# First modulation stream in tiles of 1024 columns, first softmax's factor applied to the output by ScalarE

## The chip, the core and the metric

The kernel runs on one core of a Trainium2 chip. The core has TensorE (PE in the profile), VectorE (DVE), ScalarE (ACT), GpSimd (POOL), SyncE (SP, which here only issues transfers) and 16 DMA engines that bring data from the device's memory. The engines run their own instruction streams, each in its own fixed order, and wait for one another by semaphores. Matmuls are full fp32 in value but are done as three products of rounded halves, so the three matmul lines 188, 189 and 190 always come together.

The metric is the device time of one execution in microseconds. Lower is better.

## What is computed

A trunk of two layers on 512 tokens of width 2048. The first has differential attention with eight heads, the second forgetting attention with sixteen. Each layer takes three modulation vectors of 2048 (shift, scale, gate) from a conditioning vector; the shared keys and values take two more. Cut to what the change touches:

```
c_act = silu(c)                                   # 2048
mod = c_act @ w_mod[l] + b_mod[l]                 # 3 x 2048: shift, scale, gate
mod = c_act @ w_mod_kv + b_mod_kv                 # 2 x 2048: shift, scale of the shared k, v

p = softmax(sc)                                   # per head two softmaxes, (query, key)
a = p[:, :, 0] - lam * p[:, :, 1]
o = a @ v                                         # 256 wide
o = rms_norm(o, subln_g) * (1.0 - lam_init)
o = o * silu(g)
```

## The kernel before, in words

**Projections.** The input of a layer stands transposed in 16 pairs of tiles (`hh`, `hl`: high and low half, 128 features by 512 tokens). A weight of 2048 by 512 columns is a job of eight sub-steps. For each sub-step SP loads 256 rows (`wst`), ACT rounds them to the high half (`whi`, line 108) and DVE subtracts to get the low half (`wlo`, line 109). `group` (line 318) then runs, for each sub-step, four bursts of six matmuls, one burst per accumulator bank: 32 bursts per group. With the last sub-step each bank is emptied by `evac`, right after its last burst. There are four accumulator banks, and the next group uses the same four in the same order.

**Order of the groups in the first layer.** A start phase, then `kk` and head 2's q/k group `qk[2]`, head 2's v/gate group `vg[2]`, and for heads 3 to 7 each a q/k group and a v/gate group (lines 908 to 949), then the output projection (line 1083). In time: `qk[2]` begins at 222 us, `vg[2]` ends at 329, head 4's v/gate group ends at 524, head 5's at 622, head 6's at 720, head 7's at 817. The attention of head h - 1 runs beside the groups of head h as a list of pieces; `tick` (line 302) takes one piece after each burst. `drain` takes what is left of them at once, before the first bank of a group is emptied.

**Emptying a v/gate bank** (`evac_vg`, line 716): ACT rounds v to `vh`, DVE makes `vl`, ACT takes a tanh (`th`), DVE makes `sg` (line 728). `sg` is the last reader of the bank.

**Attention of a head** (`attention_a`, line 731). `score` makes the scores of 128 queries for one of the two softmaxes, DVE adds the bias and takes the row's bound, ACT the exponent and the row sum (`e`, line 758, `rsum`). When both are there, DVE takes the reciprocals of the two sums, multiplies the second by `neglam`, multiplies the first `e` by its factor (line 765) and adds the second times its own (line 766). `e` is then transposed, either by PE (heads 0, 1 and 7) or by DVE and two trips through memory (`turn_small`, `send`, `take`). `values` multiplies by v into the bank `o`; for every two blocks of queries `norm` (line 827) copies `o` to `og`, takes the sum of squares, the reciprocal root on DVE (three rounds of tiny instructions) and scales by it and `sg` (line 839). `store` transposes `og` on PE (line 853).

**The modulation stream** (`mod_stream`, line 387) makes vectors in the background of the groups. It is a generator; `tick` takes `bg` steps of it after a burst. Here it makes four vectors, the gate of layer 0, shift and scale of the shared k and v, and the shift of layer 1, each 16 row tiles by four segments of 512 columns. One load (`ms`, line 400) brings 256 rows of a segment, two row tiles; there are two buffers, and a load is issued just ahead of the sums of the tile before it. Each step is one sum on DVE: `macc` = weights x activation (line 422 for the first row tile) or `macc` += (line 424). The sums of a stream are kept in program order. When a segment is whole, `mod_rows` (line 442) reduces over the 128 partitions: a transpose in blocks of 32 (`mturn`, line 452) and a reduction (`mred`, line 453), at step 1 of the next segment; after the fourth segment comes a matmul with ones (line 462), an add of the bias and a store, at step 5.

Steps per group before: in `qk[2]` every third burst (10 of 32), in `vg[2]` every second (16), in the q/k groups of heads 3 to 7 two of three (21), in their v/gate groups three of four (24), in the first part of the output projection one after each burst. What is left then is done at once in `open_n`.

The same generator is used a second time in layer 1 (line 1193), with segments of 512 columns.

**Order.** The kernel is written in program order, and a planner sets at build time the order in which each engine gets its instructions; it may put an instruction ahead of earlier ones that it holds to be not ready. On the chip each engine's order is then fixed.

Of the kernel before, what the change touches and what calls it, by code (L numbers as in the profile page):

```python
# [16 lines left out]
P = 128  # L17
# [107 lines left out]
def tile_yoco(  # L125
# [261 lines left out]
    def mod_stream(segs, new_stage, new_acc, nk, deep=0, new_deep=None):  # L387

        todo = [(i, r) for i in range(len(segs)) for r in range(KT // nk)]
        loaded = {}
        summed = []

        def load(k):
            i, r = todo[k]
            src, col, _ = segs[i]
            t = new_deep() if k < deep else new_stage()
            rows = src[nk * r * P : nk * (r + 1) * P, col : col + 512]
            nc.sync.dma_start(t, rows.rearrange("(k p) n -> p k n", p=P) if nk > 1 else rows)  # L400
            loaded[k] = t

        def load_upto(k):
            n = len(loads)
            while n < len(todo) and n <= (k + 7 if n < deep else k + 2 // nk):
                load(n)
                loads.append(n)
                n += 1

        loads = []  # L410
        load_upto(-1)
        for k, (i, r) in enumerate(todo):
            load_upto(k)
            if r == 0:
                acc = new_acc()
            t = loaded.pop(k)
            for kk in range(nk):
                kt = nk * r + kk
                w = t[:, kk, :] if nk > 1 else t

                if kt == 0:
                    ins = V.tensor_scalar(acc, w, cact[:, 0:1], None, op0=ALU.mult)
                else:
                    ins = V.scalar_tensor_tensor(acc, w, cact[:, kt : kt + 1], acc, op0=ALU.mult, op1=ALU.add)  # L424
                tc.keep_in_program_order(ins)
                if kt == KT - 1:
                    summed.append(segs[i][2](acc))
                if kt in (1, 5) and summed:
                    if next(summed[0], None) is None:
                        summed.pop()  # L430
                yield
        for _ in summed[0]:
            yield
# [8 lines left out]
    def mod_rows(pool, fours, dst, bias, one):  # L442
# [5 lines left out]
        def steps(n, acc):  # L448
            if n == 0:
                red.append(pool.tile([P, 64], F32, name="mred", tag="mred", bufs=2))  # L450
            t = pool.tile([P, 512], F32, name="mturn", tag="mturn", bufs=1)
            V.transpose(t, acc)
            V.tensor_reduce(
                red[0][:, 16 * n : 16 * n + 16], t.rearrange("p (j q) -> p j q", q=32), axis=mybir.AxisListType.X, op=ALU.add
            )
            if n == 3:
                row = pool.tile([64, 32], F32, name="mrow", tag="mrow", bufs=1)
                nc.sync.dma_start(row, bias.rearrange("(j q) -> j q", q=32))
            yield True
            if n == 3:  # L460
# [223 lines left out]
    for dst, src, col, bias, one in (  # L684
# [46 lines left out]
    def attention_a(h, lead=3, late=(), spread=False):  # L731
# [5 lines left out]
        def score(i, comp):  # L737
            def fn():
# [21 lines left out]
                if comp == 1:  # L760
                    r = st["rs", i]
                    V.reciprocal(r, r)
                    V.tensor_tensor(r[:, 1:2], r[:, 1:2], neglam, op=ALU.mult)
                    e0, e1 = st["e", i, 0], e
                    V.tensor_scalar(e0[:, :w], e0[:, :w], r[:, 0:1], None, op0=ALU.mult)
                    V.scalar_tensor_tensor(e0[:, :w], e1[:, :w], r[:, 1:2], e0[:, :w], op0=ALU.mult, op1=ALU.add)
            return fn
# [726 lines left out]
```

## Time and profile before

| | |
|---|---|
| median of 3 runs | 1978.77 us (1977.71 to 1979.7) |
| the profiled execution's own time | 1978.08 us |
| its span | 1976.3 us |
| granted TensorE clock | 0.994 of full speed |
| instructions on PE, DVE, ACT | 8869, 2488, 1217 |
| read from memory, written | 343.27 MB, 26.43 MB |
| `ms` loads of the first stream | 128 of 512 KB |
| `macc` sums of the first stream | 256 |

The span is the time from the first to the last instruction of the profiled execution; its own time is 1.8 us longer. PE, DVE, ACT, POOL and SP are the engines; PEld is PE's loading of weights into the array, which lies beside the matmuls. A row of a group of instructions reads: line, engine, operation, out<-in by the program's names, shapes, count | busy us in all, mean ns of one | idle us of the engine just before them, and what ended it. A row of the waits reads: who <- for whom: us in all, times, longest. A row of the timeline reads: start, duration, engine, line, operation, names, shapes, count, and in brackets the idle time before it and its releaser. A row of stretches has the stretch, its length, and for each engine the busy us and the number of instructions; then the granted clock, the share of the DMA engines' time and GB/s.

Matmuls are pipelined: one begins before the one ahead of it ends, so their durations overlap.

### The profile page before, as it was taken

What the parts mean: (1) busy time and instruction counts of PE and PEld (TensorE: products, weight loads), DVE (VectorE), ACT (ScalarE), POOL (GpSimd) and SP (SyncE); (2) the same over time, 40 slices, a digit from 0 to 9 for tenths busy, and PEclk for the clock granted to TensorE, in tenths of its full rate; (3) what the DMA queues carried; (4) which work ended last, traced back from release to release, by engine and by line L of the source; (5) the groups of instructions that cost most, each with busy time, mean ns of one, the idle gap of its engine ahead of it and who ended that gap; (6) DMA issues with size and microseconds to landing.
All of it is one profiled execution on the core that took longest, in us unless ns stands there. A gap on an engine that the chain in (4) does not pass through costs nothing.

```text
span 1976.3 us, 25268 instructions
## 1 busy us (share of the span) xinstructions
PE 1934.1 (98%) x8869; PEld 1599.5 (81%) x8869; DVE 1346.3 (68%) x2488; ACT 703.2 (36%) x1217; POOL 2.2 (0%) x10
## 2 busy tenths in 40 slices
PE   5999999999999999999999999999999999999997
PEld 4888888888888888788888888888888888888786
DVE  7885678777777778853475665666466666696557
ACT  2432445333333334431264222224334334352123
POOL 0000000000000000000000000000000000000000
PEclk8999999999999999999999999999999999999999
DMA  9993445667767677652345765664355555557422
GB/s 341 356 309 107 134 149 156 212 222 220 224 219 225 214 229 220 215 167 97 108 159 194 259 229 193 224 218 134 115 148 155 152 154 154 153 155 249 154 89 105
DMA packets 319387, 371.40 MB, mean 188 GB/s; under 512 B 57462, under 2 KB 221068, under 8 KB 318492
## 3 DMA queue, kind: packets, MB, share of 16 engines
q1 hardware_dynamic: 316880, 365.57, 57.3%
q10 hardware_dynamic: 2380, 4.21, 0.6%
q8 instruction: 70, 1.15, 0.2%
q14 instruction: 57, 0.47, 0.1%
HBM read 343.27 MB, written 26.43 MB: 187 GB/s over the span
## 4 chain that ended last, share of the span: by engine, by line
PE 88%; DVE 7%; DMA 3%; issue 1%; SPq 1%; ACT 1%; DVEq 0%; ACTq 0%
PE acc L188 26%; PE acc L189 26%; PE acc L190 25%; PE sc L188 2%; PE sc L189 2%; PE sc L190 2%; PE o L188 1%; DVE macc L424 1%; PE o L190 1%; PE o L189 1%; DMA ms<-in_kv_w_mod_dram 1%; DVE wlo L109 1%; DVE sacc L531 1%; DMA sms<-in_w_mod_dram 1%; DMA turned<-e 0%
## 5 line engine op out<-in xcount | busy, mean ns | idle before, releaser
L109 DVE TENSOR_TENSOR wlo<-wst,whi 128x1024 fp32r<-128x1024 f32 (+2 forms) x322 | 384.0, 1194 | 363.4 <-ACT whi L108 358.8
L108 ACT CAST whi<-wst 128x1024 fp32r<-128x1024 f32 (+2 forms) x322 | 331.7, 1031 | 728.0 <-PE acc L190 351.4
L188 PE MATMUL acc<-whi,hh 128*128 128x512 f32 x1232 | 483.6, 396 | 6.0 <-DVE ztmp L994 4.2
L189 PE MATMUL acc<-wlo,hh 128*128 128x512 f32 x1232 | 481.4, 391 | 0.1
L190 PE MATMUL acc<-whi,hl 128*128 128x512 f32 x1232 | 481.1, 391 | 0.0
L188 PE MATMUL acc<-hh,whi 128*128 128x512 f32 x1184 | 464.3, 392 | 2.0 <-DVE sg L728 2.0
L189 PE MATMUL acc<-hl,whi 128*128 128x512 f32 x1184 | 461.6, 390 | 0.0
L190 PE MATMUL acc<-hh,wlo 128*128 128x512 f32 x1184 | 460.7, 390 | 0.0
L188 PEld LDWEIGHTS acc<-whi,hh 128*128 128x128 f32 x1232 | 232.9, 189 | 53.2 <-DVE ztmp L994 4.7
L190 PEld LDWEIGHTS acc<-whi,hl 128*128 128x128 f32 x1232 | 231.8, 188 | 48.8
L189 PEld LDWEIGHTS acc<-wlo,hh 128*128 128x128 f32 x1232 | 232.1, 188 | 46.2 <-DVE wlo L109 0.5
L190 PEld LDWEIGHTS acc<-hh,wlo 128*128 128x128 f32 x1184 | 222.3, 188 | 47.6
L188 PEld LDWEIGHTS acc<-hh,whi 128*128 128x128 f32 x1184 | 222.5, 188 | 46.6 <-issue 2.6
L189 PEld LDWEIGHTS acc<-hl,whi 128*128 128x128 f32 x1184 | 222.6, 188 | 41.5
L424 DVE SCALAR_TENSOR_TENSOR macc<-ms,cact,macc 128x512 f32<-128x512 f32 x300 | 223.5, 745 | 34.4 <-DMA ms<-in_kv_w_mod_dram 18.6
L531 DVE SCALAR_TENSOR_TENSOR sacc<-sms,cact,sacc 128x512 f32<-128x512 f32 (+1 forms) x127 | 89.5, 704 | 5.1 <-DMA sms<-in_w_mod_dram 1.3
L758 ACT ACTIVATE e<-e,mn 128x128 f32<-128x128 f32 (+3 forms) x64 | 36.0, 563 | 114.2 <-DVE mn L754 109.9
L1298 ACT ACTIVATE eb<-eb,mnb 128x128 f32<-128x128 f32 (+1 forms) x64 | 36.1, 564 | 86.3 <-DVE mnb L1295 86.1
L754 DVE CUSTOM_DVE_ANT_0 e<-sc,bias 128x128 f32<-128x128 f32 (+3 forms) x64 | 31.0, 485 | 24.4 <-PE sc L190 24.2
L424 DVE SCALAR_TENSOR_TENSOR macc<-msk,cact,macc 128x512 f32<-128x512 f32 x60 | 45.0, 750 | 1.4
L1295 DVE CUSTOM_DVE_ANT_0 eb<-sc,biasb 128x128 f32<-128x128 f32 (+1 forms) x64 | 31.1, 486 | 17.8 <-PE sc L190 17.0
L855 ACT ACTIVATE ogT<-tr,subg 128x128 f32<-128x128 f32 x64 | 20.0, 363 | 46.1 <-PE tr L853 46.0
(262 smaller groups left out, 1759.8 us busy)
## 6 DMA issues: line engine op xcount, KB each, us to landing
wst<-in_a_w_in_dram SPq DMA_DIRECT2D x240, 256.0 KB, 3.8
ms<-in_w_mod_dram SPq DMA_DIRECT2D x64, 512.0 KB, 3.9
ms<-in_kv_w_mod_dram SPq DMA_DIRECT2D x64, 512.0 KB, 4.6
wst<-in_kv_w_dram SPq DMA_DIRECT2D x64, 512.0 KB, 3.6
sms<-in_w_mod_dram SPq DMA_DIRECT2D x56, 512.0 KB, 6.9
wst<-in_b_w_in_dram SPq DMA_DIRECT2D x112, 256.0 KB, 2.9
wst<-in_a_w_out_dram SPq DMA_DIRECT2D x32, 512.0 KB, 3.5
msk<-in_w_mod_dram SPq DMA_DIRECT2D x64, 256.0 KB, 5.5
```

The costliest lines, as they stand in the source:

```text
L108: self.nc.scalar.copy(hi[:, :, :w], st[:, :, :w])
L109: self.nc.vector.tensor_tensor(lo[:, :, :w], st[:, :, :w], hi[:, :, :w].bitcast(F32), op=ALU.subtract)
L188: PE.matmul(dst, lhs[0], rhs[0], start=start, stop=False)
L189: PE.matmul(dst, lhs[0], rhs[1], start=False, stop=False)
L190: PE.matmul(dst, lhs[1], rhs[0], start=False, stop=stop)
L424: ins = V.scalar_tensor_tensor(acc, w, cact[:, kt : kt + 1], acc, op0=ALU.mult, op1=ALU.add)
L531: V.scalar_tensor_tensor(acc, w, sc, acc, op0=ALU.mult, op1=ALU.add)
L754: V.tensor_tensor_reduce(out=e[:, :w], in0=sc[:, :w], in1=st["bias"][:, (3 - i) * P :], scale=-1.0, scalar=3.0e38, op0=ALU.add, op1=ALU.mi ...
L758: S.activation(e[:, :w], e[:, :w], AF.Exp, bias=mn, scale=-1.0, accum_out=rs)
L855: S.activation(ogT[2 * h + e][:, i * P : (i + 1) * P], pt[:, e * P : (e + 1) * P], AF.Copy, scale=subg[:, e : e + 1])
L1295: V.tensor_tensor_reduce(out=e[:, :w], in0=sc[:, :w], in1=bias[:, :w], scale=-1.0, scalar=3.0e38, op0=ALU.add, op1=ALU.min, accum_out=mn)
L1298: S.activation(e[:, :w], e[:, :w], AF.Exp, bias=mn, scale=-1.0, accum_out=rs)
```

## The change

**The stream.** All four vectors are summed in segments of 1024 columns: two segments per vector instead of four. A load brings 128 rows by 1024 columns (before 256 rows by 512), so loads stay at 512 KB and 128 in number, and each step, one per load, is one sum over 1024 columns. The reductions of a segment (two of 512 columns each) and the close of the vector come at steps 1, 4 and 7 of the next segment. The number of row tiles per load (`nk`) goes out of `mod_stream`; the number of columns, how many loads go ahead, and the steps at which reductions run become arguments. The second use of the generator keeps its 512 columns, its loads ahead (2) and its steps (1, 5).

**Steps per group.** `qk[2]` keeps its 10; `vg[2]` and all q/k and v/gate groups of heads 3 to 7 get three of eight bursts (numbers 1, 4 and 6 of each eight), 12 per group.

**The factor.** The first `e` is no longer multiplied by its reciprocal row sum. Its factor is put on `o` behind the product with v: in `norm` ACT copies each half of `o` with the factor as scale, and squares with it too. The second `e`'s factor is multiplied by the first row sum, so that the sum stands in units of the first. The reciprocals get a tile of their own.

```diff
-    def mod_stream(segs, new_stage, new_acc, nk, deep=0, new_deep=None):
+    def mod_stream(segs, new_stage, new_acc, width, ahead, late, deep=0, new_deep=None):
...
-        todo = [(i, r) for i in range(len(segs)) for r in range(KT // nk)]
+        todo = [(i, kt) for i in range(len(segs)) for kt in range(KT)]
...
-            rows = src[nk * r * P : nk * (r + 1) * P, col : col + 512]
-            nc.sync.dma_start(t, rows.rearrange("(k p) n -> p k n", p=P) if nk > 1 else rows)
...
-            while n < len(todo) and n <= (k + 7 if n < deep else k + 2 // nk):
-                load(n)
+            while n < len(todo) and n <= (k + 7 if n < deep else k + ahead):
+                i, kt = todo[n]
+                src, col, _ = segs[i]
+                t = loaded[n] = new_deep() if n < deep else new_stage()
+                nc.sync.dma_start(t, src[kt * P : (kt + 1) * P, col : col + width])
...
-                if kt in (1, 5) and summed:
+            if kt in late and summed:
...
-        def steps(n, acc):
-            if n == 0:
+        def steps(n0, n1, acc):
+            if n0 == 0:
...
-            t = pool.tile([P, 512], F32, name="mturn", tag="mturn", bufs=1)
-            V.transpose(t, acc)
...
+            for n in range(n0, n1):
+                t = pool.tile([P, 512], F32, name="mturn", tag="mturn", bufs=1)
+                V.transpose(t, acc[:, 512 * (n - n0) : 512 * (n - n0 + 1)])
...
+                yield True
+            if n1 == 4:
...
-        segs += [(src, col + 512 * f, partial(steps, f)) for f in range(4)]
+        segs += [(src, col + 1024 * f, partial(steps, 2 * f, 2 * f + 2)) for f in range(2)]
...
-        lambda: ap.tile([P, 2, 512], F32, name="ms", tag="ms", bufs=2),
-        lambda: ap.tile([P, 512], F32, name="macc", tag="macc", bufs=2),
-        2,
+        lambda: ap.tile([P, 1024], F32, name="ms", tag="ms", bufs=2),
+        lambda: ap.tile([P, 1024], F32, name="macc", tag="macc", bufs=2),
+        1024, 1, (1, 4, 7),
...
-                    r = st["rs", i]
-                    V.reciprocal(r, r)
-                    V.tensor_tensor(r[:, 1:2], r[:, 1:2], neglam, op=ALU.mult)
+                    rs = st["rs", i]
+                    r = ap.tile([P, 2], F32, name="rrec", tag="rrec", bufs=4)
+                    V.reciprocal(r, rs)
+                    V.scalar_tensor_tensor(r[:, 1:2], r[:, 1:2], neglam, rs[:, 0:1], op0=ALU.mult, op1=ALU.mult)
                     e0, e1 = st["e", i, 0], e
-                    V.tensor_scalar(e0[:, :w], e0[:, :w], r[:, 0:1], None, op0=ALU.mult)
                     V.scalar_tensor_tensor(e0[:, :w], e1[:, :w], r[:, 1:2], e0[:, :w], op0=ALU.mult, op1=ALU.add)
+                    st["r", i] = r[:, 0:1]
...
-            S.copy(og.rearrange("p r e -> p (r e)"), o)
             for r in range(2):
-                orow = o[:, r * 256 : (r + 1) * 256]
-                S.activation(orow, orow, AF.Square, accum_out=ss[:, r : r + 1])
+                orow, rr = o[:, r * 256 : (r + 1) * 256], st["r", 2 * p + r]
+                S.activation(og[:, r, :], orow, AF.Copy, scale=rr)
+                S.activation(orow, orow, AF.Square, scale=rr, accum_out=ss[:, r : r + 1])
...
-    group(vg[2], True, keep_vg, bg=lambda k: k % 2)
+    group(vg[2], True, keep_vg, bg=lambda k: k % 8 in (1, 4, 6))
...
-        group(qk[h], False, evac, bg=lambda k: k % 3 > 0)
+        group(qk[h], False, evac, bg=lambda k: k % 8 in (1, 4, 6))
...
-        group(vg[h], True, evac_rest, bg=lambda k: k % 4 > 0, after_sub=early if h == A_HEADS - 1 else None)
+        group(vg[h], True, evac_rest, bg=lambda k: k % 8 in (1, 4, 6), after_sub=early if h == A_HEADS - 1 else None)
```

More of the change, by code (lines that the diff above doesn't have):

```diff
@@ L1191, in tile_yoco @@
         steps = mod_rows(npool, fours, dst, b_mod[1, col : col + D], one)
-        segs += [(w_mod[1], col + 512 * f, partial(steps, f)) for f in range(4)]
+        segs += [(w_mod[1], col + 512 * f, partial(steps, f, f + 1)) for f in range(4)]
     background = mod_stream(
@@ L1196, in tile_yoco @@
         lambda: npool.tile([P, 512], F32, name="macc", tag="macc", bufs=2),
-        1,
+        512, 2, (1, 5),
         deep=64,
```

50 lines of the change are left out of this document (20 added, 30 removed).

## The prediction

> **What bounds the kernel now.** I read the page's busy table first, then the chain that ended last, then the busy time by stretches.
>
> ```profile
> span 1976.3 us, 25268 instructions
> ...
> PE 1934.1 (98%) x8869; PEld 1599.5 (81%) x8869; DVE 1346.3 (68%) x2488; ACT 703.2 (36%) x1217; POOL 2.2 (0%) x10
> ...
> PE 88%; DVE 7%; DMA 3%; issue 1%; SPq 1%; ACT 1%; DVEq 0%; ACTq 0%
> ```
>
> TensorE (PE) is busy 98% of the span and holds 88% of the chain. The change takes no matmul away, so all it can win is time in which PE stands still. The first modulation stream runs beside the eight attention heads of the first layer, from 222 to about 835 us; nothing of the change lies outside. The stretches below are heads 0 and 1, then four spans up to the first part of the output projection; the last row is a stretch behind the stage, of full-width matmuls alone.
>
> ```profile
> core 0: us, PE busy (x) PEld busy (x) DVE busy (x) ACT busy (x) POOL busy (x), PEclk, DMA share, GB/s
> 222.00:329.00 107.00, 107.00 (x528) 89.29 (x527) 74.39 (x191) 51.80 (x116) 0.00 (x0) 1.00 0.45 143
> ...
> 720.00:817.00 97.00, 96.58 (x448) 79.57 (x446) 82.15 (x162) 40.47 (x78) 0.00 (x0) 1.00 0.74 232
> 817.00:870.00 53.00, 51.42 (x253) 42.48 (x254) 36.54 (x100) 24.45 (x59) 0.00 (x0) 1.00 0.51 156
> sum 648.00, PE 643.41 PEld 530.87 DVE 494.05 ACT 252.94 POOL 0.00; mean PE 128.68 PEld 106.17 DVE 98.81 ACT 50.59 POOL 0.00
> ...
> 900.00:950.00 50.00, 50.00 (x222) 41.42 (x221) 18.10 (x21) 9.93 (x10) 0.00 (x0) 1.00 0.28 97
> ```
>
> PE is idle for 648.0 - 643.4 = 4.6 us of the stage. The view of PE's waits there says for whom, and PE's timeline shows where:
>
> ```profile
> PE acc L188 <- DVE sg L728: 3.8, 5, 1.8
> PE tr L853 <- DVE og L839: 0.5, 1, 0.5
> PE tr L462 <- DVE mred L453: 0.2, 1, 0.2
> ```
> ```profile
> 330.47 0.41 PE L853 MATMUL tr<-ident,og 128*128 128x128 f32 x2 [0.49 <-DVE og L839]
> ...
> 523.42 0.39 PE L189 MATMUL acc<-wlo,hh 128*128 128x512 f32 x1
> 523.65 0.39 PE L190 MATMUL acc<-whi,hl 128*128 128x512 f32 x1
> 524.49 0.47 PE L188 MATMUL acc<-hh,whi 128*128 128x512 f32 x1 [0.45 <-DVE sg L728]
> ...
> 528.48 0.47 PE L188 MATMUL acc<-hh,whi 128*128 128x512 f32 x1 [0.57 <-DVE sg L728]
> ...
> 622.52 0.47 PE L188 MATMUL acc<-hh,whi 128*128 128x512 f32 x1 [0.44 <-DVE sg L728]
> ...
> 626.51 0.47 PE L188 MATMUL acc<-hh,whi 128*128 128x512 f32 x1 [0.57 <-DVE sg L728]
> ...
> 818.34 0.47 PE L188 MATMUL acc<-whi,hh 128*128 128x512 f32 x1 [1.76 <-DVE sg L728]
> ```
>
> Matmuls start 0.23 us apart (523.42, 523.65) though each is drawn 0.39 long, so a shown gap hides another 0.16: from 523.65 to 524.49 are 0.84 us where 0.23 is normal, so 0.61 was lost for 0.45 shown. The seven waits thus cost 4.5 + 7 x 0.16 = **5.6 us**: 0.65 at 330, 1.34 at 524 and 528, 1.33 at 622 and 626, 1.92 at 818, 0.4 at L462. All of them wait for VectorE (DVE). Five are one situation: a v/gate group of eight is over, the next group wants its accumulator bank back, and DVE has not yet made `sg` out of it. So 5.6 us is about what this change can win, 0.3% of the time.
>
> [...]
>
> **Why DVE is late.** Its order is fixed and it works through it in turn, so a sum that waits for its weights holds up everything behind it.
>
> ```profile
> L424 DVE SCALAR_TENSOR_TENSOR macc<-ms,cact,macc 128x512 f32<-128x512 f32 x240 | 178.6, 744 | 32.7 <-DMA ms<-in_kv_w_mod_dram 18.6 <-DMA ms<-in_w_mod_dram 11.9
> L452 DVE STREAM_TRANSPOSE mturn<-macc 128x512 f32<-128x512 f32 x16 | 11.3, 706 | 0.1
> L453 DVE TENSOR_REDUCE mred<-mturn 128x16 f32<-128x512 f32 x16 | 10.9, 679 | 0.2
> L422 DVE TENSOR_SCALAR macc<-ms,cact 128x512 f32<-128x512 f32 x16 | 7.7, 482 | 3.2 <-DMA ms<-in_kv_w_mod_dram 2.3 <-DMA ms<-in_w_mod_dram 0.8
> ```
> ```profile
> 520.18 0.48 DVE L422 TENSOR_SCALAR macc<-ms,cact 128x512 f32<-128x512 f32 x1 [1.16 <-DMA ms<-in_kv_w_mod_dram]
> 520.58 0.70 DVE L452 STREAM_TRANSPOSE mturn<-macc 128x512 f32<-128x512 f32 x1
> 521.32 0.69 DVE L453 TENSOR_REDUCE mred<-mturn 128x16 f32<-128x512 f32 x1
> 521.92 1.22 DVE L109 TENSOR_TENSOR wlo<-wst,whi 128x1024 fp32r<-128x1024 f32 x1
> 523.05 0.42 DVE L184 TENSOR_TENSOR vl<-acc,vh 128x256 fp32r<-128x256 f32 x1
> 523.92 0.42 DVE L728 SCALAR_TENSOR_TENSOR sg<-th,acc 128x256 f32<-128x256 f32 x1 [0.45 <-ACT th L727]
> ```
>
> In the stage DVE stood 32.7 + 3.2 = 36 us waiting for `ms` loads. The six rows show one such case: 1.16 us of waiting, then the column sums (0.70 + 0.69), then a weight split (1.22), and only then the `vl` and `sg` for which PE waits until 524.49.
>
> **The change, part by part.**
>
> 1. *Sums of 1024 columns.* The 16 + 240 sums become 8 + 120. The trace has both forms at 1024 columns elsewhere:
>
> ```profile
> L1454 DVE SCALAR_TENSOR_TENSOR z<-z,mv,ln_g 128x1024 f32<-128x1024 f32 x8 | 10.1, 1275 | 0.0
> L1041 DVE TENSOR_SCALAR n<-n,mv,lrstd 128x1024 f32<-128x1024 f32 x2 | 1.6, 808 | 0.0
> ```
>
>    A pair saves 2 x 744 - 1275 = 213 ns, a first pair 2 x 482 - 808 = 156 ns: 120 x 0.213 + 8 x 0.156 = 26.8 us of DVE. The 16 transposes and 16 reductions stay. On PE's path this is worth only what it takes off the waits above.
>
> 2. *Loads.* As many, as large (512 KB), with two buffers as before; each partition gets one run of 4 KB instead of two of 2 KB. The trace has no such load, and I take the landing as it is, 3.9 and 4.6 us. A load is issued when the tile two before it is consumed. A burst of six matmuls lasts 6 x 50/222 = 1.35 us (from the row of 900 to 950). In the v/gate groups three of four bursts brought a sum; from one tile's second sum to the first of the tile after next are three such steps, 4 x 1.35 = 5.4 us, less the sum's 0.74 = 4.7. Now three of eight bursts bring one, 2 or 3 apart: at least 5 x 1.35 - 1.28 = 5.5 us. The kv loads need 4.6:
>
> ```profile
> ms<-in_w_mod_dram SPq DMA_DIRECT2D x64, 512.0 KB, 3.9
> ms<-in_kv_w_mod_dram SPq DMA_DIRECT2D x64, 512.0 KB, 4.6
> ```
>
>    So a margin of 0.1 becomes 0.9, and I expect most of the 36 us of waiting to go. SP's queue is no worse off: its wait for a sum comes later behind that sum, and `wst` loads behind it are freed earlier.
>
> 3. *Rate.* Of steps there were 10 (head 2's q/k group), 16, then 21 and 24 per head, 251 at the end of head 7's v/gate group, and the rest in the output projection. Now 10, then 12 per group: 130 at the end of head 7's q/k group, where the 128 sums and two trailing steps are done. So the stretch 222 to 329 gets 22 x 1.28 = 28 us of sums for 26 x 0.74 = 19, and with 3 us of products gone DVE there goes from 70% to about 76%, and head 7's v/gate group, in the densest stretch (82.15 of 97), loses its 24 sums, 18 us; the wait of 1.92 at 818 lies right there.
>
> 4. *Column sums.* They come now at steps 1, 4 and 7 of sixteen. Step 4 falls on the fourth-last burst of the v/gate groups of heads 2, 4 and 6 (steps 20, 68, 116), just where the banks are being emptied; heads 3 and 5 end on steps 44 to 46 and 92 to 94, which have none.
>
> 5. *The factor.* DVE loses the first product over `e`; the product with `neglam` costs what the smaller one did. ScalarE (ACT) scales 256 columns twice instead of copying 512 once, and squares with a factor.
>
> ```profile
> L765 DVE TENSOR_SCALAR e<-e,rsum 128x128 f32<-128x128 f32 (+3 forms) x32 | 12.2, 380 | 0.0
> ```
> ```profile
> L855 ACT ACTIVATE ogT<-tr,subg 128x128 f32<-128x128 f32 x64 | 20.0, 363 | 46.1 <-PE tr L853 46.0
> L835 ACT ACTIVATE o<-o 128x256 f32<-128x256 f32 x32 | 11.8, 369 | 0.9
> L832 ACT COPY og<-o 128x512 f32<-128x512 f32 x16 | 9.4, 587 | 24.0 <-PE o L190 24.0
> ```
>
>    No row has the scaled 256-column form. At least it costs what the square does (369), at most the 128-column scaled copy plus as many columns again, 363 + (587 - 369)/2 = 472. I take 472, whose kind is nearest: per norm 2 x 472 - 587 + 2 x (472 - 369) = 0.56 us more (0.15 at least), 9 us of an ACT that is busy 253 of 648. It hides behind some ten bursts between norm and `store`, but not at 330, where the last pieces are drained at once and PE already waits for `og`.
>
>    [...]
>
> *Sum.* 330: 0.65 becomes 1.2 (the 0.56, and column sums at step 20). 524/528: 1.34 becomes 0.8 (loads in time, but step 68). 622/626: 1.33 to 0. Head 6: 0 to 0.8 (step 116). 818: 1.92 to 0. L462: 0.4 to 0.3. Together 5.6 becomes 3.1: **2.5 us less**. The profiled execution took 1978.08, its span and 1.8 around it, 0.7 below the median of 1978.77; from there 1976.3.
>
> **Rivals.**
>
> *All late DVE work gone.* If the 36 us of waiting and the 39 us of sums and products (26.8 + 12.2) leave DVE early everywhere, the seven waits fall to a few tenths: 1978.8 - 5.6, **1973.2**. For it: at 622 and 818 nothing but lateness explains the wait. Against: steps 20, 68 and 116.
>
> *Slower: one long block too many.* A bank is wanted three bursts, 4.1 us, after it is full. Its chain is `vh` and `th` on ACT, `vl` and `sg` on DVE:
>
> ```profile
> L727 ACT ACTIVATE th<-acc 128x256 f32<-128x256 f32 x20 | 7.3, 385 | 14.4 <-DVE vl L184 14.4
> L183 ACT CAST vh<-acc 128x256 fp32r<-128x256 f32 x20 | 7.1, 374 | 3.5 <-PE acc L190 3.5
> ```
>
> With the 0.42 of each of the others it takes 1.6 and leaves 2.5, which one sum (1.28) and one split (1.22) fill exactly. The point is a third block between `vl` and `sg`: a second sum or the column sums cost their 1.3 to 1.4 in full. If the order puts one at each of the nine group ends of heads 3 to 7 that still have sums, that is 9 x 1.4 = 12.6, with 1.2 at 330 less the old 5.6: +8, **1987**. Against: the blocks were as dense before (three sums of 0.74 and more in the window) and two of five v/gate ends showed no wait.
>
> *Nothing gained.* DVE is no nearer to the bound than before, the loads land as late, and the longer norm shows at 330: **1979.3**.
>
> **How the numbers follow.** Forecast 0.44, its own range 1974.9 to 1978.0; all gone 0.30; nothing gained 0.14; slower 0.12. A measurement of this kernel tells about 0.2%, 4 us, from no change: faster needs under 1974.8, which is the first rival and the edge of the forecast, 0.34; slower needs over 1982.7, 0.12; between them 0.54. The range takes both faster cases and the one without gain: 1972.3 (the 5.6 and about 1 us of delays under 0.16, which don't show as idle) to 1980.5; some 0.17 lies outside.
>
> **What would show it.** 128 `macc` sums near 1.28 us; DVE's wait for `ms` under 10 us instead of 36; no wait for `sg` at the ends of heads 5 and 7; a wait of about 1 us for `og` at the end of head 2's v/gate group; ACT about 9 us busier; PE idle about 2 us in the stage. I am wrong if waits for `sg` show at ends without column sums, if `ms` is waited for as long as before, or if PE's gain or loss lies behind 870 us.

## The result

| | before | after |
|---|---|---|
| median of 6 runs each, same chip | 1980.27 us (1977.71 to 1981.72) | 1971.38 us (1970.33 to 1974.74) |
| the profiled execution's own time | 1978.08 us | 1971.12 us |
| its span | 1976.3 us | 1969.3 us |

The ratio is 0.9956, with a 95% interval of 0.9944 to 0.9968. The kernel became 8 to 9 us faster, where 2.5 had been forecast; the time lies below the lower end of the range, 1972.3. The direction was right and the size was not, and even the rival in which all late DVE work goes (5.6 us) was too small. The rest of the document is about where the other 3 us were.

The page after, busy times and chain, as the first fence of the prediction has them of before:

```profile
span 1969.3 us, 25096 instructions
...
PE 1930.4 (98%) x8869; PEld 1600.0 (81%) x8869; DVE 1321.1 (67%) x2328; ACT 708.9 (36%) x1233; POOL 2.2 (0%) x10
...
PE 94%; DVE 3%; DMA 1%; SPq 1%; issue 0%; ACT 0%; DVEq 0%; ACTq 0%
```

PE's share of the chain went from 88% to 94%; DVE's fell from 7% to 3%, DMA's from 3% to 1%. The same stretches of the stage:

```profile
222.00:329.00 107.00, 106.90 (x527) 88.89 (x526) 77.45 (x172) 51.05 (x117) 0.00 (x0) 1.00 0.59 182
...
720.00:817.00 97.00, 97.00 (x456) 80.82 (x455) 64.76 (x130) 43.33 (x86) 0.00 (x0) 1.00 0.53 165
...
sum 648.00, PE 647.71 PEld 538.54 DVE 476.52 ACT 259.52 POOL 0.00; mean PE 129.54 PEld 107.71 DVE 95.30 ACT 51.90 POOL 0.00
```

PE's idle time in the stage fell from 4.6 to 0.3 us. DVE does 17.5 us less in it and ACT 6.6 more, and the stretch from 720 to 817, head 7's two groups, DVE's densest before (82.15 of 97), is now light (64.76). Of the seven waits of PE one is left:

```profile
PE tr L847 <- DVE og L833: 0.2, 1, 0.2
```

PE's timeline has the first matmul of each head's q/k group (heads 3 to 7, then the first group of that form behind the stage). Before (those of 524.49 and 622.52 stand in the prediction):

```profile
329.14 0.39 PE L188 MATMUL acc<-hh,whi 128*128 128x512 f32 x1
...
427.35 0.39 PE L188 MATMUL acc<-hh,whi 128*128 128x512 f32 x1
...
720.15 0.39 PE L188 MATMUL acc<-hh,whi 128*128 128x512 f32 x1
...
1194.23 0.39 PE L188 MATMUL acc<-hh,whi 128*128 128x512 f32 x1
```

And after:

```profile
328.92 0.39 PE L188 MATMUL acc<-hh,whi 128*128 128x512 f32 x1
...
426.30 0.39 PE L188 MATMUL acc<-hh,whi 128*128 128x512 f32 x1
...
522.14 0.39 PE L188 MATMUL acc<-hh,whi 128*128 128x512 f32 x1
...
618.46 0.39 PE L188 MATMUL acc<-hh,whi 128*128 128x512 f32 x1
...
714.68 0.39 PE L188 MATMUL acc<-hh,whi 128*128 128x512 f32 x1
...
1185.93 0.39 PE L188 MATMUL acc<-hh,whi 128*128 128x512 f32 x1
```

From mark to mark PE has the same work, but for a piece of attention at the edges:

| stretch | before | after | gained | cost that the prediction gave the waits in it |
|---|---|---|---|---|
| head 3 | 98.21 | 97.38 | 0.83 | 0.65 (330) |
| head 4 | 97.14 | 95.84 | 1.30 | 0.61 (524) |
| head 5 | 98.03 | 96.32 | 1.71 | 1.33 (528, 622) |
| head 6 | 97.63 | 96.22 | 1.41 | 0.73 (626) |
| head 7 and behind, to 1194 | 474.08 | 471.25 | 2.83 | 2.32 (818, L462) |
| sum | | | 8.08 | 5.64 |

Every stretch won more than its shown waits cost, by 0.2 to 0.7 us. Head 6 shows it best: from 627 to 720 PE has no wait in the view of before at all, yet the head lost 0.68 more than the one wait at its start. So the stage held delays that the profile doesn't draw as idle time, because a matmul drawn 0.39 long covers the next one's coming late by up to 0.16. PE's timeline of before has most of this head's in one place, where the attention's product with v begins:

```profile
687.10 0.39 PE L190 MATMUL acc<-whi,hl 128*128 128x512 f32 x1
687.47 0.39 PE L188 MATMUL o<-vh,ah 128*128 128x256 f32 x1
...
687.81 0.39 PE L188 MATMUL acc<-whi,hh 128*128 128x512 f32 x1
688.19 0.39 PE L190 MATMUL o<-vh,al 128*128 128x256 f32 x1
```

From 687.10 to 687.47 are 0.37 us and from 687.81 to 688.19 are 0.38, where 0.23 is normal; the next matmuls, at 687.69 and 688.41, follow after 0.22 instead of the 0.12 that is normal behind 256 columns (688.41, 688.53 and 688.64 in the same timeline). That is 0.5 us lost in one place, and no bracket shows it. `ah` (ACT) and `al` (DVE) are the last steps of the chain that leads from `e` to the product, and they end at 687.41 and 688.13. In heads 3 and 4 the same matmuls start as late, the first one 0.43 us behind the one before (at 394.61 and 491.64). In the changed kernel the product loses at most 0.15 us in any of heads 3 to 6. So PE waited in a second place, at the end of a chain through DVE, which the prediction's list of waits doesn't have; in the run without the sums (e9_nosums, below) head 6 lasts 96.22 us, as in the changed kernel, and PE's one shown wait in the stage is 0.2 us for `og`.

Behind the last mark the profiled execution of the changed kernel took 1.3 us longer than the one of before (783.4 and 782.1); two other executions of it took 781.8 and 782.2, so this isn't the change's.

DVE's side, by its groups in the stage after:

```profile
L416 DVE SCALAR_TENSOR_TENSOR macc<-ms,cact,macc 128x1024 f32<-128x1024 f32 x120 | 153.0, 1275 | 24.9 <-DMA ms<-in_kv_w_mod_dram 13.1 <-DMA ms<-in_w_mod_dram 11.5
L414 DVE TENSOR_SCALAR macc<-ms,cact 128x1024 f32<-128x1024 f32 x8 | 5.9, 740 | 0.2 <-DMA ms<-in_kv_w_mod_dram 0.2
```

The sums last what was forecast, 1275 ns. But DVE still waits 24.8 us for `ms` loads, where 33.6 had been and under 10 were forecast. (The prediction's 36 us are all idle time before the sums; 33.6 of it ended with a load, and that is the figure for every run below.) So the loss went almost entirely while three quarters of the waiting stayed. Waiting on DVE and loss on PE are two things, and the experiments had to tell which part of the change took away what.

### The profile page after: what moved, and what is told of

It reads as the page before. It is cut to its first block, busy times and chain, and to the rows that moved or that the text cites. A ratio compares the mean times of both kernels' runs of the same rounds, so it can differ in the third digit from the quotient of the medians.

```text
span 1969.3 us, 25096 instructions
## 1 busy us (share of the span) xinstructions
PE 1930.4 (98%) x8869; PEld 1600.0 (81%) x8869; DVE 1321.1 (67%) x2328; ACT 708.9 (36%) x1233; POOL 2.2 (0%) x10
## 4 chain that ended last, share of the span: by engine, by line
PE 94%; DVE 3%; DMA 1%; SPq 1%; issue 0%; ACT 0%; DVEq 0%; ACTq 0%
PE acc L188 28%; PE acc L189 28%; PE acc L190 28%; PE sc L189 2%; PE sc L190 2%; PE sc L188 2%; PE o L188 1%; PE o L190 1%; PE o L189 1%; DMA sms<-in_w_mod_dram 1%; SPq L497 1%; PE tr L847 0%; DVE wlo L109 0%; DMA wst<-in_b_w_out_dram 0%; PE sc L1046 0%
## 5 line engine op out<-in xcount | busy, mean ns | idle before, releaser
L109 DVE TENSOR_TENSOR wlo<-wst,whi 128x1024 fp32r<-128x1024 f32 (+2 forms) x322 | 384.0, 1194 | 374.1 <-ACT whi L108 362.2
L416 DVE SCALAR_TENSOR_TENSOR macc<-ms,cact,macc 128x1024 f32<-128x1024 f32 (+1 forms) x180 | 197.9, 1100 | 27.9 <-DMA ms<-in_w_mod_dram 13.4
```

Of the source, the lines that this page charges most:

```text
L109: self.nc.vector.tensor_tensor(lo[:, :, :w], st[:, :, :w], hi[:, :, :w].bitcast(F32), op=ALU.subtract)
```

## The experiments

The theories at the start: PE's loss came from DVE being **late by waiting** for loads, from DVE having **too much to do** (sums and products), or from **where** the steps lay (head 7, the ends of the v/gate groups). The table gives each run against the kernel before on the same chip. Runs taken together on one chip are a series; the median of the kernel before was 1978.6 to 1979.0 in the four.

| run | median us | ratio and interval |
|---|---|---|
| e1_factor: before, factor moved | 1981.02 | 1.0018 [1.0007, 1.0030] |
| e2_stream: changed, factor not moved | 1971.60 | 0.9964 [0.9952, 0.9977] |
| e12_stream2: the same again | 1970.61 | 0.9957 [0.9945, 0.9970] |
| e3_pace: before, new steps per group | 1973.68 | 0.9974 [0.9965, 0.9983] |
| e4_width: before, 1024 columns | 1977.19 | 0.9994 [0.9985, 1.0002] |
| e5_last: changed, v/gate steps late | 1972.65 | 0.9964 [0.9950, 0.9977] |
| e6_tail: changed, sums to head 7's v/gate group | 1973.32 | 0.9971 [0.9961, 0.9981] |
| e8_changed, e13_changed2: changed | 1970.42, 1970.53 | 0.9953 [0.9941, 0.9966], 0.9956 [0.9944, 0.9969] |
| e9_nosums: changed, nearly no sums | 1969.68 | 0.9951 [0.9938, 0.9963] |
| e10_bound: changed, column sums at their steps | 1973.29 | 0.9969 [0.9957, 0.9982] |
| e11_end: before, head 7's v/gate group nearly free | 1980.47 | 1.0009 [1.0000, 1.0017] |
| e14_third: before, third `ms` buffer | 1973.26 | 0.9969 [0.9958, 0.9980] |
| e15_pace3: e3_pace with a third buffer | 1972.73 | 0.9968 [0.9956, 0.9980] |

**The factor alone.** The kernel before with the last part of the change only:

```diff
-                    V.tensor_scalar(e0[:, :w], e0[:, :w], r[:, 0:1], None, op0=ALU.mult)
...
+                    st["r", i] = r[:, 0:1]
...
-            S.copy(og.rearrange("p r e -> p (r e)"), o)
...
+                S.activation(og[:, r, :], orow, AF.Copy, scale=rr)
+                S.activation(orow, orow, AF.Square, scale=rr, accum_out=ss[:, r : r + 1])
```

> The factor on the output alone; the stream as before. Theory A (the waits went because sums no longer wait for late loads): DVE still waits some 36 us for ms, the waits for sg stay, time within 1.5 us of before, a little up at the end of head 2's v/gate group (og later by 0.56). Theory B (the waits went because DVE has less to do, wide sums and dropped products together): a third of the gain, 12 of 39 us of DVE, so 2 to 3 us off. Theory C (the waits went because steps no longer fall on the last three bursts of a v/gate group): within 1 us of before.

It was 2.1 us slower, 0.18%. PE's waits in the stage of this run:

```profile
PE acc L188 <- DVE sg L728: 3.4, 4, 1.8
PE tr L462 <- DVE mred L453: 1.9, 1, 1.9
PE acc L188 <- ACT whi L108: 0.9, 1, 0.9
```

The waits for `sg` are as before, and `mred` is now waited for 1.9 us instead of 0.2. DVE is busy 8 us less in the stage (485.63) and waits for loads 41 us instead of 33.6. Here the work taken off an engine that waits for something else came back as more waiting. The 2.1 us are not all DVE's: behind the wait for `mred` this execution shows some matmuls at half pace (last section), and its runs spread widely, from 1977.1 to 1986.5.

**The stream without the factor.** The changed kernel with the old softmax and norm, run twice, the second time beside the changed kernel itself:

```diff
+                    V.tensor_scalar(e0[:, :w], e0[:, :w], r[:, 0:1], None, op0=ALU.mult)
...
+            S.copy(og.rearrange("p r e -> p (r e)"), o)
```

> The stream alone (1024 columns, new pace, new places of the column sums); the first product over e stays on DVE. A: nearly the whole gain, 7 to 9 us off. B: two thirds, 5 to 6 us off, with some waits for sg left. C: the whole, 7 to 9 us off.

> The stream alone once more, beside the changed kernel on one chip, to size the factor: if the factor is worth something beside the new stream (12 us of DVE, a shorter way from e to ah), this is 1 to 2 us over the changed kernel; if it is worth nothing, within 0.5 us.

> The changed kernel once more, beside the stream alone on one chip: 8 to 9 us under before by every theory.

In one series 1970.61 without the factor and 1970.53 with it: beside the new stream the factor is worth nothing that can be measured. As far as these runs can tell, the stream is the whole gain.

**Steps alone and width alone.** First the old 512-column sums, both of a load in one step, with the new steps per group; then the new 1024-column sums at the old rate, with the old factor.

```diff
-                yield
+                if kk == nk - 1:
+                    yield
...
-    group(vg[2], True, keep_vg, bg=lambda k: k % 2)
+    group(vg[2], True, keep_vg, bg=lambda k: k % 8 in (1, 4, 6))
...
-        group(qk[h], False, evac, bg=lambda k: k % 3 > 0)
+        group(qk[h], False, evac, bg=lambda k: k % 8 in (1, 4, 6))
...
-        group(vg[h], True, evac_rest, bg=lambda k: k % 4 > 0, after_sub=early if h == A_HEADS - 1 else None)
+        group(vg[h], True, evac_rest, bg=lambda k: k % 8 in (1, 4, 6), after_sub=early if h == A_HEADS - 1 else None)
```

> The new pace alone: sums of 512 columns as before, the two of a load taken in one step, three steps in eight bursts; the factor as before. DVE's work is that of before. A: loads have the new lead, DVE's wait for ms falls as in the changed kernel, 6 to 8 us off. B: DVE no lighter in the middle heads, though head 7's v/gate group has no sums any more: 2 to 3 us off (the wait at 818), the waits at 524 and 622 stay. C: 6 to 8 us off.

```diff
             yield
+            if width == 1024:
+                yield
...
-    group(vg[2], True, keep_vg, bg=lambda k: k % 8 in (1, 4, 6))
+    group(vg[2], True, keep_vg, bg=lambda k: k % 2)
...
-        group(qk[h], False, evac, bg=lambda k: k % 8 in (1, 4, 6))
+        group(qk[h], False, evac, bg=lambda k: k % 3 > 0)
...
-        group(vg[h], True, evac_rest, bg=lambda k: k % 8 in (1, 4, 6), after_sub=early if h == A_HEADS - 1 else None)
+        group(vg[h], True, evac_rest, bg=lambda k: k % 4 > 0, after_sub=early if h == A_HEADS - 1 else None)
```

> The new width alone at the old pace: one sum of 1024 columns at every second of the old steps, which are as many as before per group; the factor as before. DVE has 27 us less to do. A: loads keep the old lead, DVE waits for ms as before, 0 to 2 us off. B: two thirds of what DVE loses, 4 to 5 us off. C: steps still fall on the last bursts, 0 to 2 us off.

The steps alone gave 5.2 us; the width alone 1.7, with an interval that takes in no change, though it saves DVE 20 us in the stage (473.72 against 494.05). PE's waits, of the steps alone first:

```profile
PE o L188 <- ACT ah L809: 1.3, 2, 0.7
PE tr L854 <- DVE og L840: 1.0, 2, 0.5
...
PE acc L188 <- DVE q0l L711: 0.4, 1, 0.4
```
```profile
PE acc L188 <- DVE sg L723: 2.3, 4, 0.9
PE acc L188 <- DVE q0l L705: 2.0, 3, 0.8
```

With the new steps no wait for `sg` is left and 0.4 us for `q0l`, the same kind of wait in the q/k groups, with DVE's work in the stage at 499.97 us, no less than before. (The profiled execution is the slowest of its eleven, 1976.3.) With the width alone the waits for the banks stay: `sg` 2.3, `q0l` 2.0. Less work on DVE thus doesn't buy the time by itself. What remained open: do the new steps help by where they lie, or by the time that they give the loads?

One premise of e4_width doesn't hold. Every second of the old steps in a v/gate group is two or three bursts behind the one before, just as in the changed kernel, so by the prediction's own count its loads had the new lead there and not the old one. DVE still waited 33.0 us for them, so the distance between steps alone doesn't set that wait.

**Where the steps lie.** Three runs. The changed kernel with the steps of the v/gate groups of heads 3 to 7 at the end of each eight bursts; with fewer in the q/k groups, so that sums reach head 7's v/gate group; and the kernel before with more steps early, so that this group has few:

```diff
-        group(vg[h], True, evac_rest, bg=lambda k: k % 8 in (1, 4, 6), after_sub=early if h == A_HEADS - 1 else None)
+        group(vg[h], True, evac_rest, bg=lambda k: k % 8 in (5, 6, 7), after_sub=early if h == A_HEADS - 1 else None)
```

> The changed kernel with the steps of the v/gate groups of heads 3 to 7 on the last three bursts of each eight (5, 6, 7) instead of 1, 4, 6; as many steps. Theory C (it matters which bursts carry the sums, since the banks are emptied beside the last three): waits for sg come back at the ends of heads 3 to 6, 2 to 3 us over the changed kernel. Theory A (lead of the loads): three sums in a row leave the loads 2 bursts less lead, DVE waits more for ms, 2 to 4 us over. Theory D (only the end counts: head 7's v/gate group is free of sums): within 1 us of the changed kernel.

```diff
-        group(qk[h], False, evac, bg=lambda k: k % 8 in (1, 4, 6))
+        group(qk[h], False, evac, bg=lambda k: k % 8 in (1, 5))
```

> The changed kernel with 8 steps instead of 12 in the q/k groups of heads 3 to 7 (bursts 1 and 5 of each eight), so that 110 of 130 steps are done when head 7's v/gate group begins and its 12 and the output projection carry the rest. D: the wait for sg at the end of head 7's v/gate group comes back, about 2 to 3 us over the changed kernel. C: the q/k groups gain nothing and the sums stay off the last bursts, within 1 us.

> The changed kernel itself beside the others on this chip: 7 to 9 us under before, by every theory.

```diff
-    group(vg[2], True, keep_vg, bg=lambda k: k % 2)
+    group(vg[2], True, keep_vg, bg=lambda k: k % 4 > 0)
...
-        group(qk[h], False, evac, bg=lambda k: k % 3 > 0)
+        group(qk[h], False, evac, bg=lambda k: k % 6 > 0)
```

> The kernel before, 512 columns and the old factor, with faster steps in head 2's v/gate group and the q/k groups (24 and 26 of 32), so that 252 of the 256 sums are done when head 7's v/gate group begins. D (the end of the stream counts): the wait of 1.9 us at the end of that group and what follows it go, 2.5 to 3 us under before; the waits at the ends of heads 4 and 5 stay or grow. If the pace inside the middle heads is what the changed kernel wins by: no gain, or slower.

Steps right at the banks' emptying did not bring a wait for `sg` back, though DVE waited 33.5 us for loads, as long as before; the median beside the changed kernel's is 2.2 us up, with runs that overlap. Sums in head 7's v/gate group cost 2.9 us against the changed kernel, and none of it at `sg` (the two largest of five waits):

```profile
PE tr L455 <- DVE mred L446: 0.9, 1, 0.9
PE tr L769 <- DVE e L759: 0.7, 1, 0.7
```

And the kernel before with that group freed wasn't faster: the wait at 818 went, but the middle got denser (DVE busy 316.0 us from 329 to 720, before 301.0) and DVE's waiting for loads rose to 45 us. So the place counts for something at the end, but moving the old steps in this way earned nothing.

**The floor.** The changed kernel with row tiles 1 to 15 of the first stream neither loaded nor summed:

```diff
+                if kt == 0 or width == 512:
+                    t = loaded[n] = new_deep() if n < deep else new_stage()
+                    nc.sync.dma_start(t, src[kt * P : (kt + 1) * P, col : col + width])
...
+            if w is None:
+                ins = None
...
```

> The changed kernel without the loads and sums of row tiles 1 to 15 of the first stream (so the four vectors hold one row tile's part); the column sums stay. It shows the floor: what PE loses in the stage when DVE has 150 us less to do and SP 120 loads less. If the changed kernel has already won nearly all that DVE's lateness cost, it is within 1.5 us of the changed kernel; if sums still cost PE time in losses too short to show as idle, 3 us or more under it.

```profile
sum 648.00, PE 647.66 PEld 539.23 DVE 339.47 ACT 260.32 POOL 0.00; mean PE 129.53 PEld 107.85 DVE 67.89 ACT 52.06 POOL 0.00
```

With 137 us less on DVE it is only 0.7 us faster than the changed kernel beside it (1969.68 and 1970.42). So the sums with their loads cost the kernel before 1979.0 - 1969.7 = **9.3 us**, not 5.6, and the change has taken nearly all of it. Next to nothing, 0.7 us, is left to win from this stream.

**The column sums.** In the changed kernel, with transpose and reduction kept in program order at their steps:

```diff
-                V.transpose(t, acc[:, 512 * (n - n0) : 512 * (n - n0 + 1)])
-                V.tensor_reduce(
+                tc.keep_in_program_order(V.transpose(t, acc[:, 512 * (n - n0) : 512 * (n - n0 + 1)]))
+                tc.keep_in_program_order(V.tensor_reduce(
...
```

> The changed kernel with the column sums (transposes and reductions) bound to the steps that write them, as the sums are; in the changed kernel the planner draws them some 13 us ahead, right behind the end of their segment. Theory E (the prediction was right that column sums between the emptying of banks cost PE time, and wrong that they would be there): waits for sg and og come back at the ends of the v/gate groups of heads 2, 4 and 6, 1 to 3 us over the changed kernel. Theory F (DVE has slack enough at the ends by now): within 1 us of the changed kernel, no waits for sg.

It was 2.8 us slower than the changed kernel beside it. PE's waits, and one of the places:

```profile
PE o L188 <- ACT ah L802: 3.6, 3, 1.5
```
```profile
355.36 0.39 PE L188 MATMUL o<-vh,ah 128*128 128x256 f32 x1 [1.45 <-ACT ah L802]
```

Bound to their steps, the column sums cost PE 3.6 us, in the q/k groups of heads 3, 5 and 7, some 25 us behind the group ends that the prediction had named (the three waits end at 355, 549 and 743). So the price is paid by the attention, whose `e` goes through DVE's transposes and a trip through memory before ACT can make `ah` of it, and not by the bank. In the changed kernel DVE's timeline ahead of the end of head 4 (at 522) has them elsewhere:

```profile
504.53 0.71 DVE L445 STREAM_TRANSPOSE mturn<-macc 128x512 f32<-128x512 f32 x1
...
506.14 0.68 DVE L446 TENSOR_REDUCE mred<-mturn 128x16 f32<-128x512 f32 x1
506.85 0.71 DVE L445 STREAM_TRANSPOSE mturn<-macc 128x512 f32<-128x512 f32 x1
507.60 0.69 DVE L446 TENSOR_REDUCE mred<-mturn 128x16 f32<-128x512 f32 x1
...
509.33 1.28 DVE L416 SCALAR_TENSOR_TENSOR macc<-ms,cact,macc 128x1024 f32<-128x1024 f32 x1
510.81 1.28 DVE L416 SCALAR_TENSOR_TENSOR macc<-ms,cact,macc 128x1024 f32<-128x1024 f32 x1 [0.20 <-DMA ms<-in_kv_w_mod_dram]
...
515.46 1.29 DVE L416 SCALAR_TENSOR_TENSOR macc<-ms,cact,macc 128x1024 f32<-128x1024 f32 x1 [1.69 <-DMA ms<-in_kv_w_mod_dram]
...
519.12 0.42 DVE L184 TENSOR_TENSOR vl<-acc,vh 128x256 fp32r<-128x256 f32 x1
519.99 0.42 DVE L721 SCALAR_TENSOR_TENSOR sg<-th,acc 128x256 f32<-128x256 f32 x1 [0.45 <-ACT th L720]
```

Both column sums ran at 504.5 to 508.3, as soon as their segment was whole, and `sg` is there at 520.4, well ahead of the matmul at 522.14. The fence also shows why loads are still late: the sums at 509.33 and 510.81 are 1.48 apart, not two or three bursts (2.7 or 4.1). With two buffers the load for the sum at 515.46 can only be issued when the first of them ends, at 510.6, and 4.8 us later the sum starts.

**Late loads alone.** The kernel before with a third `ms` buffer and loads going two tiles ahead, so that DVE has the same work in the same steps and only the loads come earlier; then the same in the kernel with the new steps:

```diff
-            while n < len(todo) and n <= (k + 7 if n < deep else k + 2 // nk):
+            while n < len(todo) and n <= (k + 7 if n < deep else k + 2):
...
-        lambda: ap.tile([P, 2, 512], F32, name="ms", tag="ms", bufs=2),
+        lambda: ap.tile([P, 2, 512], F32, name="ms", tag="ms", bufs=3),
```

> The kernel before with a third buffer for the loads of the first stream and loads two tiles ahead; widths, steps, places and factor as before. Theory A (sums that wait for late loads hold up DVE, and the new pace won by giving the loads more lead): DVE's wait for ms falls from 36 to under 10 us, and with it come 4 to 6 us, as the new pace alone brought. Otherwise (the pace won by where and how close the sums stand, not by the loads' lead): the waits for ms go, the time falls by less than 2 us.

> The new pace with sums of 512 columns and the old factor, and a third buffer, loads two tiles ahead. Theory A: DVE's wait for ms falls from 24 us to a few, and the time to that of the changed kernel, 7 to 9 us under before, though DVE has 39 us more to do. If DVE's work is what the wide sums win beyond the pace: it stays 5 to 6 us under before, 2 to 3 over the changed kernel.

DVE's groups in the stage with the third buffer, the page's loads, and PE's waits:

```profile
L424 DVE SCALAR_TENSOR_TENSOR macc<-ms,cact,macc 128x512 f32<-128x512 f32 x240 | 178.3, 743 | 5.4 <-DMA ms<-in_kv_w_mod_dram 2.2 <-DMA ms<-in_w_mod_dram 0.9
L422 DVE TENSOR_SCALAR macc<-ms,cact 128x512 f32<-128x512 f32 x16 | 7.7, 481 | 2.0 <-DMA ms<-in_w_mod_dram 1.6 <-DMA ms<-in_kv_w_mod_dram 0.2
```
```profile
ms<-in_w_mod_dram SPq DMA_DIRECT2D x64, 512.0 KB, 4.5
ms<-in_kv_w_mod_dram SPq DMA_DIRECT2D x64, 512.0 KB, 4.6
```
```profile
PE o L188 <- ACT ah L808: 1.0, 3, 0.4
PE tr L853 <- DVE og L839: 0.5, 1, 0.5
```

This is the run that settles where the waits for `sg` came from. The loads are no quicker (4.5 and 4.6 us; before 3.9 and 4.6) and DVE sums as much (178.3 us against 178.6), but the waiting for `ms` fell from 33.6 to 4.9 us, and with it went every wait for `sg`, the one at 818 too. The time fell by 5.8 us. That the planner put DVE's instructions into another order is not the reason: all but some 50 of the 2488 stand in the order of before, and from 512 to 560 us all of them do, where `sg` at the end of head 4 starts at 522.33 instead of 523.92. With the new steps as well the time fell by 6.3: the two do not add, so for the most part they take away the same loss. What is then left to the changed kernel, some 2 us, lies beyond pace and loads, and comes with the wide sums: 1973.68 to 1971.60 from the steps alone to steps and width in one series, each run of the second below each of the first. The changed kernel with a third buffer was not tried. No median was below the changed kernel's but that of the run that leaves the sums out.

The marks of the first table size the stage itself, in one execution of each:

| run | head 3 | head 4 | head 5 | head 6 | head 7 and behind | sum |
|---|---|---|---|---|---|---|
| before | 98.21 | 97.14 | 98.03 | 97.63 | 474.08 | 865.09 |
| e14_third | 98.55 | 96.76 | 96.73 | 96.51 | 472.33 | 860.88 |
| e4_width | 97.06 | 98.24 | 96.52 | 96.71 | 476.31 | 864.84 |
| changed | 97.38 | 95.84 | 96.32 | 96.22 | 471.25 | 857.01 |
| e9_nosums | 97.22 | 95.76 | 96.19 | 96.22 | 471.20 | 856.59 |

The third buffer wins from head 5 on, where four of the five waits for `sg` lay, and hardly anything in heads 3 and 4, where PE still waits for `ah` at the product (395 and 492 us). So late loads explain the waits for `sg` and not all of the small delays. The wide sums at the old rate come close to the changed kernel in heads 3, 5 and 6 and lose it again in head 4 and from head 7 on, where they still have sums to do; their small gain is a sum of large ones of both signs. Why head 4 loses isn't shown.

## Why the prediction was right in direction and too small

**The frame held.** PE is the bound (88% of the chain before, 94% after), the change could win only time in which PE stands still, all that it won lies ahead of the last mark, and the waits for `sg` in the kernel before came from sums that waited for loads: e14_third shows that last step by itself.

**"5.6 us is about what this change can win" failed.** That was the size of the prize, and so the ceiling of the whole sum; it measured 9.3 (e9_nosums). The seven waits were costed rightly, gap plus 0.16, but delays below 0.16 were put at about 1 us in the range, an estimate that no row gave, and at nothing in the sum, and by the table of marks those that went were 8.08 - (5.64 - 0.36) = 2.8, half a microsecond in each stretch. (0.36 is the wait that remained at the end of head 2.) They lay in good part at the product with v, which waited for the attention's chain through DVE; the prediction had PE wait for DVE at the banks and, twice, at the small matmuls of `og` and `mred`; none of its seven waits was for ACT.

PE's weight loading (PEld) comes near the size too. In the same 648 us the run without sums got through 539.23 us of it, 83.2%, and the kernel before through 530.87; at that rate the missing work takes (539.23 - 530.87)/0.832 = 10 us, an estimate that agrees with the 9.3 measured. It is rough: for e14_third, with 534.71 us, the same working gives 5.4 where the medians leave 3.6.

**"Column sums", part 4, failed.** They were put at steps 20, 68 and 116, and cost 1.2 (with the norm), 0.8 and 0.8 in the sum; measured were 0.36 at 330 and nothing at the ends of heads 4 and 6, so of the 3.1 that the sum left 0.36 remained. The step of the generator at which an instruction is issued is not its place: only the sums are held in program order, and the planner draws a column sum ahead to where its segment ends. The trace of before could have told it: in the prediction's timeline the column sums at 520.58 run ahead of the sum behind which the program issues them, which comes at 525.46. Bound to their steps they cost 2.8 us (e10_bound), about what the sum had for all three places; that is luck, since another matmul pays it, at another time.

**"Most of the 36 us of waiting to go", part 2, failed in itself.** 24.8 of 33.6 us stayed. The margin of 5.5 us was worked out between steps; the sums don't keep that distance. The loads landed in 4.5 and 4.2 us instead of 3.9 and 4.6. Yet the waiting no longer held up a bank: e5_last waits 33.5 us, as long as the kernel before, and gains 6.4. So earlier loads are enough to free the banks, as e14_third shows, but they are not the only way. That spread sums and a lighter DVE make up for a late load before a bank is wanted would explain it, but no run separates the two.

**Part 3, the rate, was right** that head 7's v/gate group would be freed and the wait at 818 go; e6_tail, with sums back in it, is 2.9 us slower than the changed kernel. But the reason was too narrow: e14_third is rid of the same wait with its sums still in that group.

**Part 1, the wide sums:** 1275 ns as forecast, 740 instead of 808 for a first one. They are worth about 2 us on top of steps or loads, and little alone.

**Part 5, the factor:** the scaled copy and square of 256 columns measured 476 and 440 ns, so 0.51 us per norm where 0.56 was taken, and ACT became 6.6 us busier instead of 9. The product with `neglam` took 219 ns, not the 159 of the smaller one.

```profile
L828 ACT ACTIVATE og<-o,rrec 128x256 f32<-128x256 f32 x32 | 15.2, 476 | 21.5 <-PE o L190 21.0
L829 ACT ACTIVATE o<-o,rrec 128x256 f32<-128x256 f32 x32 | 14.1, 440 | 0.0
```

The longer norm did not show at 330. The 12.2 us of products, of which the page's busy time shows 6 (1346.3 to 1340.3 in e1_factor; DVE's drawn durations overlap: in the prediction's timeline the sum at 520.18 is drawn 0.48 long and the next instruction starts at 520.58), are worth nothing beside the new stream (0.1 us), and alone they came with 2.1 us lost.

**The slower rival** did not come: no wait for `sg` is left in the stage, and at 519 to 520 nothing lies between `vl` and `sg`, since the column sums were drawn ahead.

## What to carry to other kernels

When an engine in fixed order delivers late, look first at what it waits for itself: here a third buffer gave half to two thirds of the gain with no work removed, while removing work alone gave 1.7 us (e4_width) or lost 2.1 (e1_factor). Size the prize by a run that leaves the suspected work out, not by the idle time that is drawn, which showed half of it (4.6 of 9.3 us): look at the distances between the starts of the matmuls too. And where a planner orders the instructions, take an instruction's place from when its data are ready, not from where the program issues it.

## What the runs showed of the hardware

In three of the executions PE ran some matmuls at about half pace behind a wait, 0.43 us apart instead of 0.23, and the wait so cost more than its length. The changed kernel's PE waits 4.23 us ahead of 1822.44, and its timeline goes on:

```profile
1817.82 0.39 PE L190 MATMUL acc<-whi,hl 128*128 128x512 f32 x1
1822.44 0.80 PE L188 MATMUL acc<-whi,hh 128*128 128x512 f32 x1 [4.23 <-DVE ztmp L988]
1823.03 0.63 PE L189 MATMUL acc<-wlo,hh 128*128 128x512 f32 x1
1823.46 0.63 PE L190 MATMUL acc<-whi,hl 128*128 128x512 f32 x1
```

Behind the gap matmuls start 0.43 us apart (1823.03, 1823.46), and the granted clock is 0.50 from 1821 to 1827 (0.93 over 1800 to 1850). The kernel before has the same wait, 4.23 us at 1830.74, matmuls 0.43 apart behind it, and a granted clock of 0.50 from 1828.5 to 1835.3. In the run with the factor alone the same came behind two shorter waits, 1.79 us at 817.66 and 1.85 at 834.17:

```profile
834.17 0.30 PE L462 MATMUL tr<-fours,mred 128*64 128x32 f32 x2 [1.85 <-DVE mred L453]
...
834.91 0.63 PE L190 MATMUL acc<-whi,hl 128*128 128x512 f32 x1
835.34 0.63 PE L188 MATMUL acc<-whi,hh 128*128 128x512 f32 x1
```

Some seven matmuls ran 0.2 us long there, about 1.5 us on top of the wait; the granted clock from 817 to 870 is 0.97. The kernel before, with one wait of 1.76 us at 818.34, kept 1.00 over the same stretch. So the half pace came once in each of two kernels behind a wait of 4.23 us, and in one execution behind the second of two waits of 1.8 us, 16 us apart; what brought the clock down isn't shown.
